# Four output products per pair, without the sums of the way back from the rotated frame, in a state-space mixer

## The chip, the cores and the metric

The kernel runs on one core of a Trainium2 chip. Its time is the device time of one execution in microseconds (us); the median of several runs is compared.

## What is computed

One sequence of 512 positions with 1024 channels passes a state-space (S5) layer, a SwiGLU feed-forward layer, a latent attention layer and a second feed-forward layer, all in float32. The change lies in the S5 layer. Cut to it:

```python
u = (h @ w_in).reshape(seq, 64 groups, 16)
a_re, a_im = decay * cos(li * step), decay * sin(li * step)
bu_re = einsum('gnk,lgk->lgn', br, u);  bu_im = einsum('gnk,lgk->lgn', bi, u)
xr, xi = associative_scan over positions of x[l] = a * x[l-1] + bu[l]      # complex
y = einsum('gkn,lgn->lgk', cr, xr) - einsum('gkn,lgn->lgk', ci, xi)
z = gelu(y + d_skip * u)
val, gate = split(z @ w_glu);  x = x + val * sigmoid(gate)
```

## The kernel before, in words

Positions are handled in blocks of `T` = 4, so that the scan runs over `C` = 128 blocks. The 64 groups of 64 states form 32 pairs that fill the 128 partitions; eight chunks t = 0..7 hold four pairs each (`PPC`). A complex recurrence is made real by turning every state into a frame that rotates with it: the inputs are turned by cosine and sine tables (`Cs`, `Sn`, made in `rotor`, L529), a real scan with the decay `RH` follows, and the result is turned back.

`s5_core` (L297) writes these steps per chunk:

- `turn_u` (L585) and `turn_w` (L576): transposes on TensorE (PE), evacuated by ScalarE (ACT) into `uT` and `WT`.
- `scan` (L594): PE makes the block inputs (L606) in two PSUM banks; VectorE (DVE) multiplies each bank by `Cs` and `Sn` (`pc`, `qc`, L612), adds them to `z` (L614, L615), scans the two parts (L617), multiplies `z` by `Cs` and `Sn` (`xpc`, `xqc`, L622) and sums these products to the real and the imaginary state `X` (L623, L624).
- `taps` (L544): small products for the part of the output that stays inside a block, evacuated by ACT into `Tb`.
- `outputs` (L626): four products of `uT` with `Tb` (L633), then two products for each of four pairs, `X` real and imaginary against the output weights `Obd` (L638). ACT applies the GELU and writes `Y` (L641). A product of two float32 operands shows as two MATMUL records in the profile.
- `coefs` (L492): DVE forms the weights `W` and `E`; ACT copies `E` into the block-diagonal `Obd` (L517), twice per chunk.
- `turn_y` (L644): `Y` is transposed on PE; ACT and DVE split it into `zh` and `zl`.
- `partial` (L653): 12 products of a finished chunk with the first gate weights, in the four `ps_g` banks.

The loop at L693 writes, for t, the steps `turn_u`, `turn_w`, `scan`, `taps` of chunk t+1, then `outputs` of t, `coefs` of t+2 and `turn_y` of t. The order in which each engine runs them is not the written one: a scheduler with a model of the times sets it when the program is built, and each engine then runs its list strictly in that order. The tiles `X`, `Obd`, `Tb`, `RH` have two buffers (chunk parity, `NB`), `z` has two, `pc` and `qc` one. The PSUM tag `x` has four banks taken in turn, so that a chunk's products wait for the readers of earlier ones. After the core, PE runs the remaining 288 gate products of the layer without a break.

Of the kernel before, what the change touches and what calls it, by code (L numbers as in the profile page):

```python
# [16 lines left out]
P = 128  # L17
# [5 lines left out]
T = 4  # L23
# [65 lines left out]
class Trunk:  # L89
# [207 lines left out]
    def s5_core(self, st):  # L297
# [44 lines left out]
        sqs = []  # L342
        for k in range(KD):
            if k % 2 == 0:
                two = cp.tile([P, 2, S], F32, name="xsq", tag=("z", "z", "pc", "qc")[k // 2], bufs=2 if k < 4 else 1)
            sqs.append(two[:, k % 2])
            nc.scalar.activation(out=sqs[k], in_=self.x[:, k], func=AF.Square)
        ups = {0: [self.ps("x") for _ in range(T)]}
# [18 lines left out]
        def tt(out, x, y, op, eng=v):  # L367
            eng.tensor_tensor(out=out, in0=x, in1=y, op=op)
# [102 lines left out]
        Wz = [lp.tile([P, 2 * PPC, 5, 16], F32, name=f"Wz{i}") for i in range(NB)]  # L471
        Tb = [lp.tile([P, 2, 2, 2, T, 16], F32, name=f"Tb{i}") for i in range(NB)]
        Obd = [lp.tile([P, 2 * PPC, T, 2, 16], F32, name=f"Obd{i}") for i in range(NB)]
        X = [lp.tile([P, 2, PPC, C], F32, name=f"X{i}") for i in range(NB)]
        RH = [lp.tile([P, PPC, C], F32, name=f"RH{i}") for i in range(NB)]
        for b in range(NB):
            g.memset(Wz[b], 0.0)
            g.memset(X[b][:, :, :, 0:1], 0.0)
            g.memset(RH[b][:, :, 0:1], 0.0)
        for z in Tb + Obd:  # L480
            g.memset(z, 0.0)

        Us, coef, states, rotors, zs, gps = {}, {}, {}, {}, [], []
# [8 lines left out]
        def coefs(t):  # L492

            bc = bcs_.pop(t)
            if t + 3 < NCT:
                load_bc(t + 3)

            def weigh(o, j, n, re, im):
                def bb(x):
                    return x.unsqueeze(2).broadcast_to([P, 2 * PPC, n, 16])  # L500

                def gg(x):
                    return x[:, 2 * t:2 * t + 2].rearrange("p a c (e j) -> p (a c e) j", e=2).unsqueeze(3).broadcast_to([P, 2 * PPC, n, 16])

                ma, mb = (cp.tile([P, 2 * PPC, n, 16], F32, name="w" + z, tag="e" + z, bufs=1) for z in "ab")
                tt(ma, bb(bc[:, j]), gg(re), M_)
                tt(mb, bb(bc[:, j + 1]), gg(im), M_)
                tt(o, ma, mb, A_)

            W = cp.tile([P, 2 * PPC, T, 16], F32, name="W", bufs=1)  # L510
            weigh(W, 0, T, GrS, GiS)
            nc.scalar.activation(out=Wz[t % NB][:, :, 1:5:2], in_=W[:, :, 0:1, :].broadcast_to([P, 2 * PPC, 2, 16]), func=AF.Copy)
            E = cp.tile([P, 2 * PPC, T + 1, 16], F32, name="E")
            weigh(E, 2, T + 1, ArS, AiN)
            for g2 in range(2):
                h = slice(64 * g2, 64 * g2 + 64)
                nc.scalar.activation(out=Obd[t % NB][h, :, :, g2], in_=E[h, :, 1:], func=AF.Copy)  # L517
            coef[t] = {"W": W, "E": E}

        def turns_of(t, o, j, start, stop):  # L520
# [73 lines left out]
        def scan(t):  # L594

            b = t % NB
            (Sn, Cs), WT, uT = rotors[t], coef[t]["WT"], states[t]
            nc.scalar.activation(out=RH[b][:, :, 1:].rearrange("p (e a) c -> p e a c", e=2),
                                 in_=rho[:, t * PPC:(t + 1) * PPC].rearrange("p (a e) -> p e a", e=2).unsqueeze(3).broadcast_to([P, 2, 2, C - 1]), func=AF.Copy)
            ps_v = [self.ps("x") for _ in range(2)]  # L600
            for q in range(2):
                for c in range(2):
                    for g2 in range(2):
                        for e in range(2):
                            h = slice(64 * e, 64 * e + 64)
                            nc.tensor.matmul(out=ps_v[e][64 * g2:64 * g2 + 64, (2 * q + c) * C:(2 * q + c + 1) * C],  # L606
                                             lhsT=WT[h, q, c, 64 * g2:64 * g2 + 64], rhs=uT[h, q, g2], start=True, stop=True)
            pc, qc = (cp.tile([P, 2, PPC, C], F32, name=n, bufs=1) for n in ("pc", "qc"))
            for e in range(2):
                vv = ps_v[e].rearrange("p (a c k) -> p c a k", a=2, c=2)  # L610
                for o, w in ((pc, Cs), (qc, Sn)):
                    tt(o[:, :, 2 * e:2 * e + 2], vv, w[:, 2 * e:2 * e + 2].unsqueeze(1).broadcast_to([P, 2, 2, C]), M_)  # L612
            z = cp.tile([P, 2, PPC, C], F32, name="z")
            tt(z[:, 0], pc[:, 0], qc[:, 1], A_)  # L614
            tt(z[:, 1], pc[:, 1], qc[:, 0], S_)  # L615
            for c in range(2):
                v.tensor_tensor_scan(out=z[:, c].rearrange("p a b -> p (a b)"), data0=RH[b].rearrange("p a b -> p (a b)"),  # L617
                                     data1=z[:, c].rearrange("p a b -> p (a b)"), initial=0.0, op0=M_, op1=A_)
            n = C - 1
            xc, xs = (cp.tile([P, 2, PPC, C], F32, name="x" + m, tag=m, bufs=1) for m in ("pc", "qc"))  # L620
            for o, w in ((xc, Cs), (xs, Sn)):
                tt(o[:, :, :, :n], z[:, :, :, :n], w[:, :, :n].unsqueeze(1).broadcast_to([P, 2, PPC, n]), M_)  # L622
            tt(X[b][:, 0, :, 1:], xc[:, 0, :, :n], xs[:, 1, :, :n], S_)  # L623
            tt(X[b][:, 1, :, 1:], xc[:, 1, :, :n], xs[:, 0, :, :n], A_)  # L624

        def outputs(t):  # L626

            b = t % NB
            uT = states.pop(t)
            ps_y = self.ps("x")  # L630
            for q in range(2):
                for g2 in range(2):
                    nc.tensor.matmul(out=ps_y.rearrange("p (q e j g k) -> p q g e j k", q=2, e=2, j=T, g=2)[:, q, g2], lhsT=uT[:, q, g2],  # L633
                                     rhs=Tb[t % NB][:, q, g2].rearrange("p e j k -> p (e j k)"), start=q == 0 and g2 == 0, stop=False, skip_group_check=True)
            for q in range(2):
                for e in range(2):
                    for c in range(2):
                        nc.tensor.matmul(out=ps_y[:, (2 * q + e) * P:(2 * q + e + 1) * P], lhsT=X[b][:, c, 2 * e + q],  # L638
                                         rhs=Obd[b][:, 4 * q + 2 * c + e].rearrange("p j g k -> p (j g k)"), start=False, stop=c == 1, skip_group_check=True)
            Y = cp.tile([P, T, PPC, 32], F32, name="Y", bufs=1)  # L640
            nc.scalar.activation(out=Y.rearrange("p j a k -> p a j k"), in_=ps_y.rearrange("p (a j k) -> p a j k", a=PPC, j=T), func=AF.Gelu_apprx_tanh)  # L641
            states[t] = Y
# [36 lines left out]
        rotor(0)  # L679
        taps(0)  # L680
        scan(0)
        rotor(1)
        coefs(1)

# [6 lines left out]
            whole_turns(t)  # L691
            rotor(t)
        for t in range(NCT):  # L693
            for f, d in ((turn_u, 1), (turn_w, 1), (scan, 1), (taps, 1), (outputs, 0), (coefs, 2), (turn_y, 0)):
                if 0 <= t + d < NCT:
                    f(t + d)
                if f is scan and t in (1, 3):
# [461 lines left out]
```

## Time and profile before

| | before |
|---|---|
| median of 3 runs | 1229.52 us (1227.26 to 1230.77) |
| the profiled execution | 1228.52 us, of which the span from the first to the last instruction is 1226.7 us |
| PE matmul busy | 1182.0 us (96%) |
| PE weight load busy | 959.8 us (78%) |
| DVE busy | 664.2 us (54%) |
| ACT busy | 489.2 us (40%) |
| mean granted TensorE clock | 0.979 of full speed |

The shares are means over stages of quite different kinds. The S5 core lies in about the first 200 us of the span; the rest is mostly feed-forward and attention, where PE is busy throughout. Windows of the trace are therefore read stage by stage, and the waits of PE within them.

### The profile page before, as it was taken

To read this page: it belongs to the slowest core of one execution; us is meant where nothing else is said; L and a number is where in the kernel's file an instruction comes from. 1 tells how busy PE (TensorE), PEld (TensorE's weight loads), DVE (VectorE), ACT (ScalarE), POOL (GpSimd) and SP (SyncE) were. 2 spreads that over 40 slices of the span, in tenths; PEclk is the share of its full clock that TensorE was granted. 3 is DMA by queue.
4 is the path that set the end of the run, shared out by engine and by line. 5 is a ranking of instruction groups with operands and counts; after the bars stand their busy time and mean duration, and the time that the engine had idled before them with its cause. 6 is when DMAs were issued, how large, how long until landed. Compare 5 with 4: busy or idle time off the path is not lost.

```text
span 1226.7 us, 15533 instructions
## 1 busy us (share of the span) xinstructions
PE 1182.0 (96%) x6133; PEld 959.8 (78%) x6136; DVE 664.2 (54%) x1194; ACT 489.2 (40%) x821; POOL 137.2 (11%) x149
## 2 busy tenths in 40 slices
PE   7977999999999999999999898999999999999998
PEld 6766777888888888888878676667888888888887
DVE  7797894357444444333358767744844444443221
ACT  7646444254232232233245766644432332322110
POOL 0300000030000000000234445432100000000000
PEclk9978799999999999999999899999999999999999
DMA  6210012323333233333222101103233232333331
GB/s 230 69 27 27 28 36 86 103 86 104 91 98 103 92 97 99 95 95 95 86 88 67 37 2 41 52 2 103 86 103 103 87 103 91 99 99 103 120 114 46
DMA packets 31896, 100.96 MB, mean 82 GB/s; under 512 B 3664, under 2 KB 4688, under 8 KB 31824
## 3 DMA queue, kind: packets, MB, share of 16 engines
q1 hardware_dynamic: 31680, 99.97, 26.2%
q8 instruction: 48, 0.79, 0.3%
q14 instruction: 24, 0.20, 0.1%
q10 hardware_dynamic: 144, 0.00, 0.0%
HBM read 97.86 MB, written 2.10 MB: 81 GB/s over the span
## 4 chain that ended last, share of the span: by engine, by line
PE 83%; DVE 9%; ACT 4%; issue 2%; POOL 1%; DMA 1%; SPq 0%; DVEq 0%; ACTq 0%
PE ps_ps L155 20%; PE ps_ps L154 20%; PE ps_ps L153 19%; PE ps_s L965 2%; PE ps_x L153 2%; PE ps_x L155 2%; PE ps_x L154 2%; PE ps_a L153 2%; PE ps_a L154 2%; PE ps_a L155 2%; DVE wl L142 1%; PE ps_x L638 1%; PE ps_g L153 1%; PE ps_x L606 1%; PE ps_po L1002 1%
## 5 line engine op out<-in xcount | busy, mean ns | idle before, releaser
L141 ACT ACTIVATE wh<-w 128x1024 fp32r<-128x1024 f32 (+3 forms) x193 | 191.3, 993 | 548.0 <-PE ps_ps L154 351.0
L142 DVE TENSOR_TENSOR wl<-w,wh 128x1024 fp32r<-128x1024 f32 (+3 forms) x193 | 221.9, 1151 | 212.8 <-ACT wh L141 212.7
L153 PE MATMUL ps_ps<-fh,wh 128*128 128x512 f32 x704 | 274.2, 390 | 0.0
L155 PE MATMUL ps_ps<-fh,wl 128*128 128x512 f32 x704 | 273.4, 389 | 0.0
L154 PE MATMUL ps_ps<-fl,wh 128*128 128x512 f32 x704 | 273.4, 389 | 0.0
L154 PEld LDWEIGHTS ps_ps<-fl,wh 128*128 128x128 f32 x704 | 132.1, 188 | 28.1 <-issue 0.5
L153 PEld LDWEIGHTS ps_ps<-fh,wh 128*128 128x128 f32 x704 | 132.1, 188 | 27.6 <-issue 0.5
L155 PEld LDWEIGHTS ps_ps<-fh,wl 128*128 128x128 f32 x704 | 132.1, 188 | 27.5
L153 PE MATMUL ps_ps<-ah,wh 128*128 128x512 f32 x352 | 136.9, 389 | 0.0
L154 PE MATMUL ps_ps<-al,wh 128*128 128x512 f32 x352 | 136.9, 389 | 0.0
L155 PE MATMUL ps_ps<-ah,wl 128*128 128x512 f32 x352 | 136.9, 389 | 0.0
L743 DVE TENSOR_TENSOR ut<-ps_ps,rstd 128x512 f32<-128x512 f32 x44 | 30.4, 691 | 127.8 <-PE ps_ps L155 127.8
L263 POOL TENSOR_TENSOR acc<-acc,sq 128x512 f32<-128x512 f32 x21 | 30.5, 1452 | 564.6 <-ACT sq L258 316.0
L153 PEld LDWEIGHTS ps_ps<-ah,wh 128*128 128x128 f32 x352 | 66.1, 188 | 13.8
L154 PEld LDWEIGHTS ps_ps<-al,wh 128*128 128x128 f32 x352 | 66.1, 188 | 13.8
L155 PEld LDWEIGHTS ps_ps<-ah,wl 128*128 128x128 f32 x352 | 66.1, 188 | 13.5
L740 DVE TENSOR_TENSOR gt<-ps_ps,rstd 128x512 f32<-128x512 f32 x44 | 30.4, 691 | 83.2 <-PE ps_ps L155 83.1
L973 POOL TENSOR_SCALAR p<-p,sm 128x128 f32<-128x128 f32 (+2 forms) x48 | 45.8, 960 | 70.6 <-DVE sm L971 59.3
L965 PE MATMUL ps_s<-kT,qT 96*128 96x384 f32 (+3 forms) x128 | 46.6, 466 | 1.5 <-ACT p L970 1.5
L970 ACT ACTIVATE p<-ps_s,mx 128x128 f32<-128x128 f32 (+3 forms) x64 | 33.4, 525 | 22.8 <-DVE mx L968 18.6
L168 ACT ACTIVATE ah<-ut 128x512 fp32r<-128x512 f32 x44 | 27.9, 634 | 30.7 <-DVE ut L744 30.7
L968 DVE TENSOR_REDUCE mx<-ps_s 128x1 f32<-128x128 f32 (+3 forms) x64 | 30.8, 486 | 15.1 <-PE ps_s L966 14.6
(384 smaller groups left out, 1756.1 us busy)
## 6 DMA issues: line engine op xcount, KB each, us to landing
w<-w_gu SPq DMA_DIRECT2D x88, 512.0 KB, 3.5
w<-w_down SPq DMA_DIRECT2D x32, 512.0 KB, 3.5
w<-w_glu SPq DMA_DIRECT2D x12, 512.0 KB, 3.5
w<-w_down SPq DMA_DIRECT2D x16, 384.0 KB, 3.1
w<-w_in SPq DMA_DIRECT2D x7, 512.0 KB, 3.6
w<-w_o SPq DMA_DIRECT2D x6, 512.0 KB, 3.2
x<-xT SPq DMA_DIRECT2D x8, 256.0 KB, 6.0
bc<-ssm_bc SPq DMA_DIRECT2D x8, 256.0 KB, 2.8
```

Of the source, the lines that this page charges most:

```text
L141: nc.scalar.activation(out=wh[:, c], in_=w[:, c], func=AF.Copy)
L142: nc.vector.tensor_tensor(out=wl[:, c], in0=w[:, c], in1=wh[:, c].bitcast(F32), op=ALU.subtract)
L153: nc.tensor.matmul(out=out, lhsT=lh, rhs=rh, start=start, stop=False)
L154: nc.tensor.matmul(out=out, lhsT=lh, rhs=rl, start=False, stop=False)
L155: nc.tensor.matmul(out=out, lhsT=ll, rhs=rh, start=False, stop=stop)
L263: nc.gpsimd.tensor_tensor(out=acc, in0=acc, in1=sq, op=ALU.add)
L740: v.tensor_tensor(out=gt, in0=pss[0], in1=rstd, op=ALU.mult)
L743: v.tensor_tensor(out=ut, in0=pss[1], in1=rstd, op=ALU.mult)
L965: nc.tensor.matmul(out=ps, lhsT=qT[:, i * P:n], rhs=kT[:, 0:n], start=True, stop=False)
L968: v.reduce_max(out=m1, in_=ps, axis=AX.X, negate=True)
L970: nc.scalar.activation(out=pb, in_=ps, func=AF.Exp, bias=m1, accum_out=s1)
L973: eng.tensor_scalar(out=pb, in0=pb, scalar1=s1, scalar2=None, op0=M_)
```

## The change

The two DVE sums that made `X` from `xpc` and `xqc` are gone. The products of `z` with the cosine (`XC`) and the sine (`XS`) go to PE as they are, and `outputs` makes four products per pair: the real part of `XC` and the imaginary part of `XC`, with the weights that `X` had; the real part of `XS` with the weights of the imaginary part; the imaginary part of `XS` with the negated weights `On`, a new tile that ACT copies from `E` with scale -1 (twice per chunk). `XC` and `XS` have one buffer each, `z` has one instead of two, and the turning back is a step of its own, `rotate`, written after `outputs` of the chunk before. Two more fills on GpSimd (POOL) zero `On`.

```diff
+        On = [lp.tile([P, PPC, T, 2, 16], F32, name=f"On{i}") for i in range(NB)]
-        X = [lp.tile([P, 2, PPC, C], F32, name=f"X{i}") for i in range(NB)]
+        XC, XS = (lp.tile([P, 2, PPC, C], F32, name=m) for m in ("XC", "XS"))
...
                 nc.scalar.activation(out=Obd[t % NB][h, :, :, g2], in_=E[h, :, 1:], func=AF.Copy)
+                nc.scalar.activation(out=On[t % NB].rearrange("p (a e) j g k -> p a e j g k", e=2)[h, :, :, :, g2],
+                                     in_=E.rearrange("p (a c e) j k -> p c a e j k", a=2, c=2)[h, 0, :, :, 1:], func=AF.Copy, scale=-1.0)
...
-            z = cp.tile([P, 2, PPC, C], F32, name="z")
+            z = cp.tile([P, 2, PPC, C], F32, name="z", bufs=1)
...
-            xc, xs = (cp.tile([P, 2, PPC, C], F32, name="x" + m, tag=m, bufs=1) for m in ("pc", "qc"))
-            for o, w in ((xc, Cs), (xs, Sn)):
-                tt(o[:, :, :, :n], z[:, :, :, :n], w[:, :, :n].unsqueeze(1).broadcast_to([P, 2, PPC, n]), M_)
-            tt(X[b][:, 0, :, 1:], xc[:, 0, :, :n], xs[:, 1, :, :n], S_)
-            tt(X[b][:, 1, :, 1:], xc[:, 1, :, :n], xs[:, 0, :, :n], A_)
+            states[t] = (uT, z)
+
+        def rotate(t):
+            (Sn, Cs), n = rotors[t], C - 1
+            states[t], z = states[t]
+            for o, w in ((XC, Cs), (XS, Sn)):
+                tt(o[:, :, :, 1:], z[:, :, :, :n], w[:, :, :n].unsqueeze(1).broadcast_to([P, 2, PPC, n]), M_)
...
-                    for c in range(2):
-                        nc.tensor.matmul(out=ps_y[:, (2 * q + e) * P:(2 * q + e + 1) * P], lhsT=X[b][:, c, 2 * e + q],
-                                         rhs=Obd[b][:, 4 * q + 2 * c + e].rearrange("p j g k -> p (j g k)"), start=False, stop=c == 1, skip_group_check=True)
+                    r = 4 * q + e
+                    for i, (lhs, rhs) in enumerate(((XC[:, 0], Obd[b][:, r]), (XC[:, 1], Obd[b][:, r + 2]), (XS[:, 0], Obd[b][:, r + 2]), (XS[:, 1], On[b][:, 2 * q + e]))):
+                        nc.tensor.matmul(out=ps_y[:, (2 * q + e) * P:(2 * q + e + 1) * P], lhsT=lhs[:, 2 * e + q],
+                                         rhs=rhs.rearrange("p j g k -> p (j g k)"), start=False, stop=i == 3, skip_group_check=True)
...
-            for f, d in ((turn_u, 1), (turn_w, 1), (scan, 1), (taps, 1), (outputs, 0), (coefs, 2), (turn_y, 0)):
+            for f, d in ((turn_u, 1), (turn_w, 1), (scan, 1), (taps, 1), (outputs, 0), (rotate, 1), (coefs, 2), (turn_y, 0)):
```

Because the scheduler sets the order, the lists of the engines differ in more than the diff shows. Three places matter below.

The first is ACT around the GELU of chunk 0 (`Y`, L641 before, L649 now); `Obd` is refilled for chunk 2, `WT` is the input of the scan of chunk 2. Before:

```order
L598 ACTIVATE RH_486<-dr 128x4x127
L641 ACT_TABLE_LOAD
L641 ACTIVATE Y<-ps_x 128x4x4x32
L517 ACTIVATE Obd_481<-E 64x32x16 x2
L591 ACTIVATE uT<-ps_x 128x512
L582 ACTIVATE WT<-ps_x 128x512
L168 ACTIVATE zh_890<-ps_x 128x512
```

Now:

```order
L595 ACTIVATE uT<-ps_x 128x512
L602 ACTIVATE RH_488<-dr 128x4x127
L519 ACTIVATE Obd_481<-E 64x32x16 x2
L649 ACT_TABLE_LOAD
L649 ACTIVATE Y<-ps_x 128x4x4x32
L520 ACTIVATE On_483<-E 64x16x16 x2
L586 ACTIVATE WT<-ps_x 128x512
L168 ACTIVATE zh_900<-ps_x 128x512
```

`uT` moved ahead of the end of `outputs`; the refill of `Obd`, which needs `outputs` to be over with the old one, moved ahead of the GELU; the pair of `On` copies stands between `Y` and `WT`.

The second is PE around the outputs of chunk 3 (L633 and L638 before, L640 and L646 now), with the two halves of the scan inputs of chunk 4 (L606 before, L610 now). Before:

```order
L606 MATMUL ps_x<-uT,WT 64x128 x8
L521 MATMUL ps_x<-counts,turned 128x512
L153 MATMUL ps_g<-zh_1287,wh 128x512 x4
L633 MATMUL ps_x<-Tb_480,uT 128x8x16 x4
L638 MATMUL ps_x<-Obd_482,X_484 128x128 x8
L606 MATMUL ps_x<-uT,WT 64x128 x8
```

Now:

```order
L610 MATMUL ps_x<-uT,WT 64x128 x8
L525 MATMUL ps_x<-counts,turned 128x512
L153 MATMUL ps_g<-zh_1309,wh 128x512 x4
L640 MATMUL ps_x<-Tb_480,uT 128x8x16 x4
L646 MATMUL ps_x<-Obd_482,XC 128x128 x2
L646 MATMUL ps_x<-Obd_482,XS 128x128
L646 MATMUL ps_x<-On_484,XS 128x128
L646 MATMUL ps_x<-Obd_482,XC 128x128 x2
L646 MATMUL ps_x<-Obd_482,XS 128x128
L610 MATMUL ps_x<-uT,WT 64x128 x8
```

The second half of the scan inputs now stands behind 7 of the 16 output products, where it stood behind all 8.

The third is DVE between the input of chunk 4's scan (`scan`) and its turning back (`rotate` now). Before:

```order
L368 TENSOR_TENSOR E<-wa,wb 128x640
L368 TENSOR_TENSOR pc<-ps_x,Cs 128x2x256
L368 TENSOR_TENSOR qc<-ps_x,Sn 128x2x256
L368 TENSOR_TENSOR wa<-bc,GrS 128x512
L368 TENSOR_TENSOR wb<-bc,GiS 128x512
L368 TENSOR_TENSOR z<-pc,qc 128x512 x2
L142 TENSOR_TENSOR wl<-w,wh 128x512
L169 TENSOR_TENSOR zl_1436<-ps_x,zh_1435 128x512
L617 SCALAR_TENSOR_TENSOR z<-RH_485,z 128x512 x2
```

Now:

```order
L368 TENSOR_TENSOR E<-wa,wb 128x640
L368 TENSOR_TENSOR wa<-bc,GrS 128x512
L368 TENSOR_TENSOR wb<-bc,GiS 128x512
L368 TENSOR_TENSOR pc<-ps_x,Cs 128x2x256
L368 TENSOR_TENSOR qc<-ps_x,Sn 128x2x256
L368 TENSOR_TENSOR z<-pc,qc 128x512 x2
L621 SCALAR_TENSOR_TENSOR z<-RH_487,z 128x512 x2
L368 TENSOR_TENSOR XC<-z,Cs 128x8x127
L368 TENSOR_TENSOR XS<-z,Sn 128x8x127
L169 TENSOR_TENSOR zl_1464<-ps_x,zh_1463 128x512
```

Four operations (`wa`, `wb`, `wl`, `zl`) no longer stand between the second `pc` and the scan.

## Rows read from the trace of the kernel before

**Rows 1.** By stretch: length, busy us (x count) PE, PEld, DVE, ACT, POOL, PEclk, DMA.
```profile
63.00:139.00 76.00, 63.29 (x661) 53.89 (x661) 64.65 (x88) 41.05 (x92) 0.00 (x0) 0.80 0.09 25
139.00:157.90 18.90, 15.62 (x157) 13.16 (x156) 17.33 (x24) 12.80 (x26) 0.00 (x0) 0.82 0.09 29
157.90:200.00 42.10, 41.23 (x361) 34.49 (x362) 31.86 (x55) 19.08 (x40) 0.00 (x0) 1.00 0.13 39
280.00:500.00 220.00, 220.00 (x973) 182.15 (x972) 109.19 (x134) 69.07 (x85) 0.00 (x0) 1.00 0.31 97
```
**Rows 2.** Waits of PE from 63 to 157.9: us in total, times, longest.
```profile
PE ps_x L648 <- ACT Y L641: 4.4, 3, 2.7
PE ps_x L558 <- ACT uT L591: 3.1, 1, 3.1
PE ps_x L606 <- ACT WT L582: 2.5, 2, 1.6
PE ps_x L580 <- ACT ab L540: 2.2, 1, 2.2
...
PE ps_x L633 <- DVE qc L368: 0.4, 1, 0.4
```
**Rows 3.** Stretches at the lower clock: the first of five, and their sum.
```profile
68.40:78.20 9.80, 9.80 (x119) 9.54 (x119) 9.01 (x15) 5.56 (x16) 0.00 (x0) 0.50 0.21 55
...
sum 36.80, PE 36.36 PEld 32.89 DVE 32.76 ACT 13.89 POOL 0.00; mean PE 7.27 PEld 6.58 DVE 6.55 ACT 2.78 POOL 0.00
```
**Rows 4.** The chain of waits, chunks 1 to 6: start us, us, what.
```profile
79.50 1.12 DVE z L617
...
81.29 1.28 ACT L641
...
89.97 2.62 PE ps_x L638 x14
...
116.48 1.80 PE ps_x L638 x16
...
128.54 2.35 PE ps_x L638 x16
...
151.08 3.02 PE ps_x L638 x16
...
170.84 1.29 DVE X L368 x2
```
**Rows 5.** PE in order of time: start us, us, what, around two chunks' outputs.
```profile
77.11 2.57 PE L638 MATMUL ps_x<-Obd,X 128*128 128x128 f32 x16
79.52 0.60 PE L590 MATMUL ps_x<-ctab,U 128*128 128x128 f32 x4
...
116.32 1.95 PE L638 MATMUL ps_x<-Obd,X 128*128 128x128 f32 x16
118.10 0.60 PE L580 MATMUL ps_x<-ctab,W 128*128 128x128 f32 x4
```
**Rows 6.** Groups from 60 to 190: count, busy us, mean ns, idle before.
```profile
L368 DVE TENSOR_TENSOR X<-xpc,xqc 128x508 f32<-128x508 f32 x16 | 10.2, 681 | 0.0
...
L517 ACT ACTIVATE Obd<-E 64x512 f32<-64x512 f32 x12 | 7.5, 623 | 0.1
...
L512 ACT ACTIVATE Wz<-W 128x256 f32<-128x256 f32 x6 | 2.5, 410 | 0.0
```
**Rows 7.** DVE in order of time, chunk 4's scan (in brackets: idle before).
```profile
131.97 0.69 DVE L368 TENSOR_TENSOR pc<-ps_x,Cs 128x512 f32<-128x512 f32 x1 [2.86 <-PE ps_x L606]
...
133.17 0.68 DVE L368 TENSOR_TENSOR wa<-bc,GrS 128x512 f32<-128x512 f32 x1
133.77 0.69 DVE L368 TENSOR_TENSOR wb<-bc,GiS 128x512 f32<-128x512 f32 x1
```
**Rows 8.** POOL's last fill of the core, and ACT's first copy into that tile.
```profile
40.78 1.85 POOL L481 MEMSET Obd<- 128x1024 f32 x2
...
44.80 1.28 ACT L517 ACTIVATE Obd<-E 64x512 f32<-64x512 f32 x2
```

More of the change, by code (lines that the diff above doesn't have):

```diff
@@ L344, in s5_core @@
             if k % 2 == 0:
-                two = cp.tile([P, 2, S], F32, name="xsq", tag=("z", "z", "pc", "qc")[k // 2], bufs=2 if k < 4 else 1)
+                two = cp.tile([P, 2, S], F32, name="xsq", tag=("z", "U", "pc", "qc")[k // 2], bufs=2 if k // 2 == 1 else 1)
             sqs.append(two[:, k % 2])
@@ L477, in s5_core @@
             g.memset(Wz[b], 0.0)
-            g.memset(X[b][:, :, :, 0:1], 0.0)
             g.memset(RH[b][:, :, 0:1], 0.0)
-        for z in Tb + Obd:
+        for z in (XC, XS):
+            g.memset(z[:, :, :, 0:1], 0.0)
+        for z in Tb + Obd + On:
             g.memset(z, 0.0)
@@ L618, in scan @@
                                      data1=z[:, c].rearrange("p a b -> p (a b)"), initial=0.0, op0=M_, op1=A_)
-            n = C - 1
-            xc, xs = (cp.tile([P, 2, PPC, C], F32, name="x" + m, tag=m, bufs=1) for m in ("pc", "qc"))
-            for o, w in ((xc, Cs), (xs, Sn)):
-                tt(o[:, :, :, :n], z[:, :, :, :n], w[:, :, :n].unsqueeze(1).broadcast_to([P, 2, PPC, n]), M_)
-            tt(X[b][:, 0, :, 1:], xc[:, 0, :, :n], xs[:, 1, :, :n], S_)
-            tt(X[b][:, 1, :, 1:], xc[:, 1, :, :n], xs[:, 0, :, :n], A_)
+            states[t] = (uT, z)
[4 more added lines that the diff above has]
+                tt(o[:, :, :, 1:], z[:, :, :, :n], w[:, :, :n].unsqueeze(1).broadcast_to([P, 2, PPC, n]), M_)
         def outputs(t):
@@ L681, in s5_core @@
         scan(0)
+        rotate(0)
         rotor(1)
```

## Prediction

> **What bounds the kernel now.** Read the busy time by stretch first [rows 1]. From 280 to 500 us PE is busy for 220 of 220 us: there only PE's own work counts, and the engines' lists of those stages are the same but for a few rows. The S5 core is different. From 63 to 157.9 us PE is busy for 63.29 + 15.62 = 78.9 of 94.9 us and its clock is low in between; from 157.9 to 200 it is busy for 41.23 of 42.1 at full clock, and so on to the end of the layer. So the core has two parts: one with waits up to 157.9, and one after it in which PE already has its work end to end. DVE is close to full as well: 17.33 of 18.9 us just before 157.9.
>
> Next, who holds PE in the first part [rows 2]. The nine rows of that view come to 15.8 us; ACT ends 14.9 of them in six rows (the GELU `Y`, `uT`, `WT`, and `ab` of the rotor), DVE 1.0 in three, of which 0.4 is the longest. PE also runs at half speed in five stretches, 36.8 us together, whose clock is about 0.50, i.e. 1.2 of 2.4 GHz [rows 3]; that costs 36.8 / 2 = 18.4 us of work. Each such stretch follows a wait of PE on ACT.
>
> Last, the chain of waits [rows 4]. It passes through the output products L638 of chunks 1, 2, 3 and 4, goes from there through ACT (table load, `Y`, `Obd`, `WT`) to the scan inputs of the chunk after next, and back. The sums that the change drops stand on it once, at 170.84. The reader should see that DVE is busy but not what the others wait for, and that the output products, which are doubled, are.
>
> **The change, part by part.** *Dropped sums.* Sixteen additions of 128x508 at 10.2 us of busy time; an operation of this size starts the next one 0.60 later (133.17 and 133.77), so DVE loses 16 x 0.6 = 9.6 us of work [rows 6, 7]. `XC` and `XS` have the shape of the old products and cost the same.
>
> *Added products.* Eight per chunk, two records each: 16 records took 118.10 - 116.32 = 1.78 us at full clock [rows 5]. So 8 x 1.78 = 14.2 us of PE. At half clock the chain shows 3.02 for the same 16, mixed; the added ones stand last in their group, where the clock has mostly risen, so I take 1.8. The bounds of a group are 1.8 and 3.0.
>
> *Added copies.* Two `On` copies per chunk of 64x256. The nearest rows are `Wz`, 128x256 at 0.41, and `Obd`, 64x512 at 0.62 [rows 6]; the length of a partition's row is that of `Wz`, so 0.41 each, 0.8 a chunk, at most 1.2. In chunks 1, 2 and 4 they lie between `Y` and what PE waits for.
>
> *Fills.* Two more on POOL, half as long as `Obd`'s, which take 1.85 for two and end at 42.6; ACT comes to that kind of copy at 44.80 [rows 8], so a microsecond more is covered. Without that cover the first scan would start up to 1 us later.
>
> *Order and buffers.* `XC` and `XS` have one buffer: `rotate` of t+1 waits for the outputs of t. Behind it on DVE stand `W`, `zl` and the next `pc`, for which `turn_w`, the gate products and the next scan wait. `z` with one buffer costs nothing, since its only reader, `rotate`, is ahead of the next `z` on the same engine.
>
> *The sum, first part (to 157.9), by chunk.* Chunk 0: the outputs ended at 79.52, and ACT, which waited for the scan of chunk 1 (to 80.6), began its table load at 81.29 [rows 4, 5]. They now end 1.8 + 0.5 later (the four transposes of `U` moved ahead of them), at 81.8, or 0.5 past that; `On` adds 0.8, and `uT`, now ahead, gives back about 0.5, a copy between `Wz` and `Obd` in time: +0.8. Chunk 1: 1.8 + 0.8 = +2.6, all on the chain. Chunk 2: the same 2.6, and 24 instead of 20 gate products ahead of the next scan's inputs, 4 x 220 / 973 = 0.9 [rows 1]: +3.5. Chunk 3: the second half of the scan inputs now waits for 7 products instead of 8, -0.2; on DVE `wa`, `wb`, `wl` and `zl` no longer follow the second `pc` but fill its wait of 2.86 or come later, 4 x 0.6 [rows 7]: -2.4. Chunk 4: +2.6. Together 0.8 + 2.6 + 3.5 - 2.6 + 2.6 = **+6.9 us** at the point where PE's unbroken work begins, and from there on it is the same work but for three chunks' added products.
>
> *Second part.* Chunks 5, 6 and 7 add 3 x 1.78 = 5.3 us to an engine that has 42.10 - 41.23 = 0.9 us left [rows 1]: **+4.4 us**. DVE's gain of 4 x 1.2 there (four chunks from 139 on) is not what PE waits for.
>
> Sum: 6.9 + 4.4 = 11.3 on the profiled execution's 1228.5, or 1239.8; I take **1239.5**, since small orders that I could not follow (a scheduler that packs its lists again) rather give than take. The profiled execution is 1.0 below the median of the three runs.
>
> A rule speaks against the second part. The Trainium skill's page Perfetto Trace Analysis, section Identifying the Most-Contended Engine, says that matmul busy time is a bad measure of what PE has left, and that the busy share of the weight loads is the one to read. By it PE has room: 34.49 of 42.1 us, 82%, so that the 5.3 us would fit and the sum would be 1235.4. The trace disagrees: in the feed-forward stretch, where matmuls follow each other without a gap, the same share is 182.15 of 220, 83% [rows 1], so 82% is full here and the rule gets no chance of its own.
>
> **The rivals.** *A, the added products lie in PE's waits up to 157.9.* PE has 15.8 us of waits there and needs 5 x 1.8 = 9.0. Then only the second part is paid: 1228.5 + 4.4 = 1232.9. For it: the room is there. Against it: the waits come after the outputs, on ACT's `Y` and `WT`, which start only when the outputs end; the added products push a wait, they don't fill it. It decides if ACT's start is set by something else than the outputs, as it is in chunk 0.
>
> *B, DVE was the bound: faster.* DVE has only 1.6 us free from 139 to 157.9 [rows 1], and 9.6 us fall away. If DVE set the pace of all chunks, 9.6 would come off and 4.4 be added: 1223.3. It decides if PE's products wait for `pc`/`qc` or `X` rather than for ACT. Against it: DVE ends only 1 us of PE's waits [rows 2], and itself waits for PE's scan inputs (2.86 at 131.97) [rows 7].
>
> *C, PE keeps its clock.* If the denser work of PE spared two of the five stretches at the lower clock, 2 x 36.8 / 5 / 2 = 7.4 us would come back: 1232.1; all five, 18.4, give 1221.1. Against it: each stretch starts after a wait on ACT [rows 2, 3] that the change lengthens. The Trainium skill's page TensorE: Matmul & The Clock Gate, Part 1, says that the throttled clock is the default and that activity releases it. By that rule more products in a gap would help; the trace shows all five stretches behind gaps that the change leaves.
>
> *D, the single buffer bites.* The scan of chunk 1 ends at 80.6 and the lengthened outputs of chunk 0 at 81.8 [rows 4, 5], so `rotate` waits there by 1 us; if it waits like that or by 2 in the chunks that follow, beyond what the sum holds, and one more stretch at the lower clock follows in chunk 6, 36.8 / 5 / 2 = 3.7 us, the time is near 1228.5 + 11.3 + 3.7 + 2 = 1245.5.
>
> That the sums are not really dropped is no case: the list of DVE has 16 fewer additions.
>
> **How the numbers follow.** About 0.3% (3.7 us) is what a measurement of this kernel can tell from no change, so 1225.8 to 1233.2 counts as the same. Forecast 0.52 (its own range 1234 to 1245); A 0.17, B 0.08, C 0.08, D 0.15. Faster: B and a third of C, 0.11. Same: A and a third of C, 0.20. Slower: the rest, 0.69. The range 1228 to 1247 takes in A, the forecast, D and half of C; it leaves out B, the rest of C and a tail above, under 0.2. With `On` at 0.62 and a group at 3.0 in the three chunks of the chain, the sum would be 1.2 + 3.6 higher, 1244.6, which the range holds.
>
> **What the profile would show.** L646 with 256 records and 1.8 us more per group; PE's matmul and load time each longer. The waits of PE on `Y`, `WT` and `uT` no smaller; five stretches at the lower clock. DVE busy 9 to 10 us less, with new waits: `XC` on the output products, `pc` and `zl` longer. PE's unbroken work begins near 165 instead of 157.9, and the layer's last gate product ends some 11 us later; behind it all stages last as long as before. I am wrong if the waits of PE shrink by more than 5 us, if fewer stretches are slow, or if the end of the layer moves by less than 4 us.

## The result, and the profile after

The changed kernel took **1244.48 us** (median of 4 runs, 1239.11 to 1249.12) beside 1228.76 for the kernel before (4 runs, 1227.26 to 1230.77): ratio 1.0132, 95% interval 1.0108 to 1.0156. Measured again beside other kernels (run e5) it was 1244.81 us, ratio 1.0140 (1.0122 to 1.0157). The forecast was 1239.5, its range 1228 to 1247. The sign and the range held; the terms behind the number, as the experiments show, did not all hold, and part of the agreement is luck.

The profiled execution of the changed kernel took 1242.62 us (span 1240.8), 14.1 more than that of before. First the busy time by stretch: us, then PE, weight loads, DVE, ACT, POOL busy with the number of instructions, PE's granted clock, DMA share, GB/s.

```profile
63.00:139.00 76.00, 61.62 (x634) 52.74 (x633) 58.90 (x79) 40.65 (x91) 0.00 (x0) 0.84 0.08 22
139.00:173.00 34.00, 27.74 (x347) 24.85 (x346) 26.31 (x34) 20.65 (x45) 0.00 (x0) 0.83 0.07 25
173.00:216.00 43.00, 42.84 (x343) 38.42 (x342) 26.43 (x46) 20.21 (x41) 0.00 (x0) 0.97 0.13 40
296.00:516.00 220.00, 220.00 (x972) 182.16 (x971) 107.59 (x132) 69.42 (x86) 0.00 (x0) 1.00 0.32 98
```

Beside [rows 1]: in the feed-forward stretch PE is busy for 220 of 220 us, as before. PE's unbroken work, which began at 157.9, now begins at 165.8, but at half the clock until 175 (below). The first product of the feed-forward layer moved from 255.38 to 269.75, by 14.4: the whole difference lies ahead of it.

Not all of that belongs to the change. ACT's first copy of `GrS`, ahead of anything that the diff touches in the core, started at 37.59 before and at 40.18 after, because two loads took longer (`ctab` by 1.2, `w` by 1.5 us). In e5, the same kernel, it started at 39.24, and in e1 at 38.11: this is scatter between executions. So I count from that copy to the first feed-forward product, once for each kernel (the columns of the view above):

```profile
37.59:255.38 217.79, 200.24 (x1622) 166.97 (x1623) 158.14 (x227) 109.94 (x222) 4.41 (x13) 0.91 0.19 55
```

```profile
40.18:269.75 229.57, 208.78 (x1752) 178.93 (x1751) 150.04 (x211) 116.37 (x238) 5.34 (x15) 0.92 0.17 52
```

217.79 became 229.57: **+11.8 us**. The table divides this time for each profiled execution. PE's busy time and granted clock were read in 200 equal slices of it; "work" is the sum of busy x clock, "low clock" the sum of busy x (1 - clock), "waits" the time less the busy time. The three add up to the time, to rounding.

```
kernel                       its run   time    work   low clock   waits
before                       1228.5   217.8   181.9     18.3      17.5
after                        1242.6   229.6   192.0     16.8      20.8
e5  after again              1245.2   233.2   190.9     23.5      18.8
e1  before, products twice   1236.5   225.9   193.0     16.9      16.0
e2  before, no sums          1222.0   211.2   180.5     12.7      17.9
e3  order alone              1230.8   218.5   182.1     20.0      16.3
e4  after, no On             1247.3   235.2   192.7     23.9      18.6
e6  e4 with two buffers      1234.9   225.5   191.5     19.8      14.2
e7  e6, rotate in scan       1232.5   221.8   192.2     15.1      14.5
e8  coef. sums on GpSimd     1228.0   217.9   183.7      9.3      25.0
e9  before, no coef. sums    1223.6   211.2   180.8     16.4      14.0
e10 before, twice late       1230.0   219.3   186.5     15.0      17.8
e11 work in the gaps         1229.5   217.5   184.2     16.2      17.0
e12 three buffers of RH      1226.9   216.6   180.8     18.1      17.7
```

Each row is one execution and can lie off the median of its kernel: e4's is the longest of its six (1234.7 to 1247.3), e2's too, and e1's (1236.5) is near the shortest of 1236.2 to 1243.6. From before to after, work grew by 10.1 and waits by 3.3; the low clock cost 1.5 less in this run, but 5.2 more in e5. The growth of the work goes with the added products, but it is less than the 14.2 us that the prediction counted for them; the measure is a rough one (in e11 added transposes are busy for 6.3 us and raise it by 2.3). The groups of the output products from 60 to 215 us (group, count, busy us, mean ns of one, idle before):

```profile
L646 PE MATMUL ps_x<-Obd,XC 128*128 128x128 f32 x128 | 20.6, 286 | 0.0
L646 PE MATMUL ps_x<-On,XS 128*128 128x128 f32 x64 | 12.8, 283 | 0.0
L646 PE MATMUL ps_x<-Obd,XS 128*128 128x128 f32 x64 | 12.8, 282 | 0.0
```

They are 256 records where there were 128, four kinds per pair. Next the waits of PE from 63 to 175 (us in total, times, longest):

```profile
PE ps_x L656 <- ACT Y L649: 8.2, 3, 3.0
PE ps_x L640 <- DVE qc L368: 3.3, 2, 2.5
PE ps_x L584 <- DVE zl L169: 2.8, 1, 2.8
PE ps_x L610 <- ACT WT L586: 2.4, 4, 0.8
PE ps_x L584 <- ACT ab L544: 2.2, 1, 2.2
PE ps_x L562 <- ACT uT L595: 0.8, 1, 0.8
```

Against [rows 2], `Y` rose from 4.4 to 8.2, and DVE, which ended 1.0 us of PE's waits, now ends 6.3, 2.8 of it by `zl` ahead of the transposes of `W`. On DVE itself the new wait is the one on the single buffer (in brackets: idle before, and what ended it):

```profile
160.84 1.22 DVE L368 TENSOR_TENSOR XC<-z,Cs 128x1016 f32<-128x1016 f32 x1 [1.08 <-PE ps_x L646]
...
178.50 1.22 DVE L368 TENSOR_TENSOR XC<-z,Cs 128x1016 f32<-128x1016 f32 x1 [1.92 <-PE ps_x L646]
```

And between the outputs of chunks 4 and 5, where chunk 6's scan inputs are made, stands a stretch at the lower level, 1.2 GHz, that the kernel before did not have: ten microseconds with PE at work for 9.2 (columns as in the first fence).

```profile
165.00:175.00 10.00, 9.21 (x114) 8.90 (x115) 6.35 (x10) 4.03 (x13) 0.00 (x0) 0.50 0.01 2
```

### The profile page after: what moved, and what is told of

The parts are those of the page before. It is cut to its first block, busy times and chain, and to the rows that moved or that the text cites. A ratio compares the mean times of both kernels' runs of the same rounds, so it can differ in the third digit from the quotient of the medians.

```text
span 1240.8 us, 15799 instructions
## 1 busy us (share of the span) xinstructions
PE 1190.7 (96%) x6264; PEld 972.0 (78%) x6264; DVE 658.9 (53%) x1178; ACT 494.5 (40%) x837; POOL 135.6 (11%) x151
## 4 chain that ended last, share of the span: by engine, by line
PE 85%; DVE 7%; ACT 4%; issue 1%; POOL 1%; DMA 1%; SPq 0%; DVEq 0%; ACTq 0%
PE ps_ps L153 19%; PE ps_ps L155 19%; PE ps_ps L154 19%; PE ps_s L974 2%; PE ps_x L646 2%; PE ps_x L153 2%; PE ps_x L155 2%; PE ps_x L154 2%; PE ps_a L153 2%; PE ps_a L154 2%; PE ps_a L155 2%; PE ps_po L1011 1%; PE ps_g L153 1%; PE ps_x L610 1%; PE ps_a L959 1%
## 5 line engine op out<-in xcount | busy, mean ns | idle before, releaser
L142 DVE TENSOR_TENSOR wl<-w,wh 128x1024 fp32r<-128x1024 f32 (+3 forms) x193 | 224.8, 1166 | 215.9 <-ACT wh L141 215.7
L154 PEld LDWEIGHTS ps_ps<-al,wh 128*128 128x128 f32 x352 | 66.1, 188 | 13.8
```

Source lines behind the costliest of these rows:

```text
L142: nc.vector.tensor_tensor(out=wl[:, c], in0=w[:, c], in1=wh[:, c].bitcast(F32), op=ALU.subtract)
L154: nc.tensor.matmul(out=out, lhsT=lh, rhs=rl, start=False, stop=False)
```

## The experiments

All ratios are against the kernel before, measured beside each; microseconds are the ratio less 1, times 1228, and differ from the difference of the medians by up to 0.9. One thing holds for all of them: a scheduler writes each engine's list from its own simulated times, so that an edit comes with a list that is packed again. One list matters below, ACT's, and it is read from the traces.

**e1, the products alone.**

```diff
-  Obd[..] <- E
-  for c in (0, 1):        ps_y += X[c] . Obd[4q+2c+e]
+  Obd[..] <- 0.5 * E
+  for c in (0, 1, 0, 1):  ps_y += X[c] . Obd[4q+2c+e]
```

> The kernel before, with each of its eight output products per chunk made twice (Obd halved by the scale of its copy, so that two of them add up to one); the sums, the order of the loop and the buffers stay as they were, and no On copy is made. Theory (the added products are the cost: 1.8 us in chunks 1, 2 and 4, 0.5 in chunk 0, 4.4 us in chunks 5 to 7): +9.5 to +10.5 us over before, about 1239. Rival buffer and order (the products mostly fit in PE's waits, and the wait of XC on the outputs, the moved rotate and the On copies make the rest): about +4.4, 1233. Rival clock (the added cost is the slow stretch in chunk 6, which the new order brought): under +6, and no stretch at 0.50 behind 165 us.

Measured: 1238.5 us, ratio 1.0090 (1.0069 to 1.0112), **+11.1 us**. The theory's band was 9.5 to 10.5; both rivals, at +4.4 and under +6, are outside the interval (8.5 to 13.8). By the table, whose execution shows 8.1 of it, PE's work grew by 11.1; 1.5 of it came back in waits and 1.4 through the clock. A low stretch came at the same place here too (159 to 169 us, clock 0.54), without the new order: the order does not make it.

**e2, the sums alone.**

```diff
-  xpc = z * Cs ; xqc = z * Sn
-  X[0] = xpc[0] - xqc[1] ; X[1] = xpc[1] + xqc[0]
+  xqc = z * Sn ; X = z * Cs
```

> The kernel before without the two sums per chunk: the product with the cosine goes straight into X, the product with the sine is made and not read (this leaves the sums out of the computation). Nothing else is changed: eight products, order, two buffers of X. Theory (DVE is busy, but its sums are not what the others wait for): -2.5 to +0.5 us against before. Rival B (DVE sets the pace): -6 to -10 us.

Measured: 1218.77 us, ratio 0.9921 (0.9906 to 0.9936), **-9.7 us**. My theory falls; the number is rival B's. But B's mechanism (DVE holds PE) is not what the table shows: PE's waits are 17.9 beside 17.5, its work is 180.5, and 5.6 us come from the clock (this execution, at 1222.0, shows 6.6 of the 9.7). The place is the stretch from 95 to 111 us. Before, and then e2:

```profile
95.00:111.00 16.00, 12.79 (x106) 10.05 (x108) 12.12 (x15) 12.85 (x30) 0.00 (x0) 0.79 0.07 17
```

```profile
95.00:111.00 16.00, 15.24 (x196) 12.18 (x193) 14.47 (x21) 13.71 (x35) 0.00 (x0) 1.00 0.13 35
```

Before, PE works 12.8 of 16 us at a mean clock of 0.79; in e2 15.2 at 1.00. ACT's list differs there. Before, ACT in order of time, then what PE did:

```profile
98.14 1.28 ACT L539 ACT_TABLE_LOAD   x1
...
100.59 0.58 ACT L168 ACTIVATE zh<-ps_x 128x512 fp32r<-128x512 f32 x1
...
101.55 0.60 ACT L591 ACTIVATE uT<-ps_x 128x512 f32<-128x512 f32 x1
```

```profile
102.20 1.90 PE L558 MATMUL ps_x<-E,Wz 64*64 64x64 f32 x32 [3.06 <-ACT uT L591]
```

The sine table load and `Sn`, `RH`, `zh`, `ab` stand ahead of `uT`; PE waits 3.06 for `uT`, and the third of the five stretches at the lower clock follows. In e2 the same engine reads:

```profile
96.39 0.60 ACT L168 ACTIVATE zh<-ps_x 128x512 fp32r<-128x512 f32 x1
96.89 0.59 ACT L591 ACTIVATE uT<-ps_x 128x512 f32<-128x512 f32 x1
...
99.94 1.28 ACT L539 ACT_TABLE_LOAD   x1
```

Here `zh`, `uT` and `U` stand ahead of the table load, at 96.89 instead of 101.55, and from 87 to 110 us PE has no wait over 0.4. So the scheduler, with the sums gone, wrote another list. How much of the 9.7 is that list and how much DVE's time, this run does not tell.

**e9, as much off DVE at another place.**

```diff
-  tt(mb, bc[j+1], im) ; tt(o, ma, mb, add)
+  tt(o, bc[j+1], im)
```

> The kernel before without the sums of the coefficients: the second product goes straight into W and E (this leaves those two sums per chunk out of the computation). It takes 0.60 + 0.73 us per chunk off DVE, 8 in 8 chunks, slightly more than the sums of the way back (9.6), but not between scan and products, and with nothing put on GpSimd. If DVE's load is what counts: -6 to -10 us against before, the clock at 0.985 or more as in e2_before_no_sums. If the place of the sums counts (between z and the output products): -3 to +1 us, the clock near 0.979.

Measured: 1224.59 us, ratio 0.9969 (0.9958 to 0.9979), **-3.8 us**, clock by run 0.979 to 0.984. The interval, -5.2 to -2.6, leaves out "DVE's load is what counts" and reaches the edge of "the place of the sums counts" (-3 to +1). Its list of ACT is of e2's kind (`uT` at 95.89, the table load at 98.95), so that this list and 10.6 us less of DVE are here together worth 3.8, and cannot by themselves account for the 9.7 of e2. In the profiled execution the waits are 3.5 lower, and the low clock costs 1.9 less.

**e8, the same load moved to GpSimd.**

```diff
-  tt(o, ma, mb, add)                 # DVE
+  gpsimd.tensor_tensor(o, ma, mb, add)
```

> The kernel before, with the two sums of the coefficients per chunk (W 128x512, E 128x640) made by GpSimd in place of DVE; the core's sums and eight products stay. It takes off DVE 8 x (0.6 + 0.73) = 10.6 us, about as much as the sums of the way back, and adds no PE work. If what counts is DVE's load and not that chain of sums: -6 to -10 us against before, 1218 to 1222, under both kernels. If the sums counted because z, X and the products follow each other, or GpSimd is slow at it and W comes late: -1 to +5 us.

Measured: 1227.59 us, ratio 0.9991 (0.9981 to 1.0002): no change that can be told, at the edge of the second expectation. It is not that nothing happened: the clock by run rose to 0.984 to 0.989, and in the table the low clock costs 9.0 less while PE's waits are 7.5 longer. Nor was DVE's load lowered, as the run was to do: DVE did not get the time back. Two products and the sums of e8 on DVE, then GpSimd's sums beside them:

```profile
98.05 2.12 DVE L368 TENSOR_TENSOR xpc<-z,Cs 128x1016 f32<-128x1016 f32 x1
100.09 1.21 DVE L368 TENSOR_TENSOR xqc<-z,Sn 128x1016 f32<-128x1016 f32 x1
...
102.69 2.64 DVE L368 TENSOR_TENSOR X<-xpc,xqc 128x508 f32<-128x508 f32 x2
```

```profile
97.78 1.31 POOL L508 TENSOR_TENSOR W<-wa,wb 128x512 f32<-128x512 f32 x1 [10.08 <-PE ps_x L580]
102.84 1.94 POOL L508 TENSOR_TENSOR E<-wa,wb 128x640 f32<-128x640 f32 x1 [3.75 <-DVE wb L368]
```

The product with the cosine takes 2.12 where the one with the sine behind it takes 1.21, and two sums take 2.64 where one group takes 1.29 in [rows 4]; both lie beside a sum of GpSimd, of which the second takes 1.94. The Trainium skill's page Perfetto Trace Analysis, section Optimizing Scalar/DVE Operations, says that GpSimd and DVE share a read port of SBUF, so that work moved between them may not help; these rows agree.

**e3, the order alone.**

```diff
-  scan: ... X <- sums            # inside scan, X in two buffers
+  rotate(t+1): X <- sums         # behind outputs(t), X and z in one buffer
```

> The order and the buffers of the changed kernel, with the arithmetic of the kernel before: the way back and its sums stand in rotate behind the outputs, X and z have one buffer, eight products per chunk, no On copies. Theory: the order gives +0.9 (24 gate products), -0.5 (uT) and about -2 in chunk 3, but the sums now stand behind the outputs on DVE, four more instructions of 0.6 between XC and W: -2 to +3 us against before. Rival buffer and order: +5 to +9 us, most of what the changed kernel lost.

Measured: 1227.45 us, ratio 0.9998 (0.9986 to 1.0010), **-0.2 us**. With eight products the moved way back and its single buffer cost nothing. Taken alone this would have closed the case of the buffer; e6 opens it again.

**e5, the changed kernel again,** no edit.

> The changed kernel as it is, measured again beside the others of this call. All theories: its first four runs lay between 1239.1 and 1249.1, so a median of 1240 to 1247, and a mean granted clock of 0.972 to 0.983 by run, as there.

Measured as given above; its clock by run was 0.972 to 0.975. It was measured beside e6 and e7. The next run, e4, was measured on another chip, so that e4 is compared with these through the ratios to the kernel before.

**e4, without On.**

```diff
-  On <- -1 * E ; XS = z * Sn ; fourth product XS[1] . On
+  XS[0] = z[0] * Sn ; XS[1] = (z[1] * -1) * Sn ; fourth product XS[1] . Obd[r]
```

> The changed kernel without the On copies: the sign is put into XS by writing its second half as (z times -1) times Sn, in one instruction, so XS takes two instructions of 128x508 in place of one of 128x1016, and the fourth product reads Obd. Four products per pair as in the changed kernel. Theory (0.8 us of On lie on the chain in chunks 0, 1, 2 and 4): -2.5 to -3.5 us against the changed kernel, +8 to +13 against before, with the products' cost left. Rival (the copies lie in waits of ACT): within 1 us of the changed kernel.

Measured: 1240.67 us (1234.69 to 1247.25), ratio 1.0102 (1.0075 to 1.0128). Against e5 that is 0.0038 or **-4.7 us**, with an uncertainty of about 3.9 (both half-widths, squared and added). Against the first measurement of the changed kernel (1.0132) it is -3.7, with an uncertainty of 4.4, so that no gain at all lies inside it too. It fits the theory and the 3.2 of the prediction, but the rival's "within 1 us" is not ruled out; and the traces do not show where the gain lies, since e4's execution, its longest, took longer than both of the changed kernel.

**e6, two buffers.**

```diff
-  XC, XS: one buffer ; WT: two
+  XC, XS: two buffers ; WT: one
```

> The changed kernel without On (sign put into XS) and with two buffers of XC and XS, so that rotate of a chunk does not wait for the outputs of the chunk before (WT gets one buffer to make the space). The order of the loop stays. Theory buffer (the single buffer holds DVE and undoes what the dropped sums give): 1230 to 1235, some 7 us under the version without On and with one buffer (1240.7). Theory products (with the products doubled PE is late whatever DVE does): within 2.5 us of 1240.7, since XC waited for the products by 3.0 us in all in the changed kernel's trace.

Measured: 1234.62 us, ratio 1.0046 (1.0032 to 1.0061); against e4 0.0056 or **-6.9 us**, uncertainty about 3.7. The theory of the buffer holds, the other is out. DVE's waits from 62 to 200 (us in total, times, longest), e4 and then e6, which has none at `XC`:

```profile
DVE pc L368 <- PE ps_x L607: 15.2, 8, 3.8
...
DVE XC L368 <- PE ps_x L644: 5.6, 3, 2.2
```

```profile
DVE wl L142 <- ACT wh L141: 10.4, 6, 3.7
DVE pc L368 <- PE ps_x L607: 6.2, 7, 1.8
```

5.6 us of waiting at `XC`, and 15.2 instead of 6.2 at `pc` behind it. Part of this can be that e4's execution was its longest (12.4 us above e6's, where the ratios make it 6.9). And the scheduler's list for ACT turns with the buffer. ACT in e4, and the wait of PE that follows:

```profile
107.08 1.28 ACT L540 ACT_TABLE_LOAD   x1
...
109.34 0.60 ACT L168 ACTIVATE zh<-ps_x 128x512 fp32r<-128x512 f32 x1
...
110.29 0.63 ACT L592 ACTIVATE uT<-ps_x 128x512 f32<-128x512 f32 x1
```

```profile
110.72 1.11 PE L581 MATMUL ps_x<-ctab,W 128*128 128x128 f32 x4 [4.20 <-DVE zl L169]
```

ACT in e6:

```profile
100.40 0.60 ACT L168 ACTIVATE zh<-ps_x 128x512 fp32r<-128x512 f32 x1
100.90 0.59 ACT L592 ACTIVATE uT<-ps_x 128x512 f32<-128x512 f32 x1
...
102.96 1.28 ACT L540 ACT_TABLE_LOAD   x1
```

e4 has the table load ahead of `zh` and `uT`, and PE waits 4.20 for `zl`, which DVE makes from `zh`; e6 has it behind them, and no such wait. The changed kernel has e4's kind (table load 102.06, `zh` 103.85, a wait of 2.80).

**e7, the arithmetic alone.**

```diff
-  rotate(t+1) behind outputs(t)
+  XC, XS written inside scan, as X was
```

> The kernel of e6_no_on_two_buffers with rotate back in the place of the kernel before, inside scan, ahead of taps and outputs: what is left of the change is its arithmetic alone (sums dropped, sixteen products). If the two parts add up as they measured alone (products +10.4, sums -9.3): 1229 +- 2. Theory products (the gain of the sums does not stand once the products are doubled): 1236 to 1241. Theory order (the moved rotate is the loss): at least 6 us under e6_no_on_two_buffers.

Measured: 1232.37 us, ratio 1.0039 (1.0023 to 1.0054), **+4.8 us** (2.8 to 6.6) over before; against e6 0.9, within its uncertainty: the order is no loss here either. (e6 and e7 keep XS in two instructions and one buffer of WT.) The interval leaves out 1236 and more, "the gain of the sums does not stand". Adding e1 and e2 gives +1.4, 3.4 less than measured, but with the uncertainties of all three runs (3.7 together) this does not show that the parts fail to add up. Most of the sums' gain, 11.1 - 4.8 = 6.3 of 9.7 (uncertainty 3.3), stands beside sixteen products.

**e10, the late products alone.**

```diff
+  if t >= 5: as e1, else as before
```

> The kernel before with its output products made twice in chunks 5, 6 and 7 only (Obd halved there). The prediction's second term says 3 x 1.78 - 0.9 = +4.4 us, all of it PE time in a stretch where PE has no waits; that leaves 10.4 - 4.4 = 6.0 us for chunks 0 to 4. Rival (the late chunks' products fit, the whole 10.4 us came from chunks 0 to 4): under +2 us. Rival (the late chunks pay more, a further stretch at the lower clock): +7 or more.

Measured: 1230.31 us, ratio 1.0018 (1.0006 to 1.0031), **+2.2 us** (0.7 to 3.8): between the forecast's 4.4 and the rival's "under 2". The time of the whole program misleads here. Up to the outputs of chunk 5 each engine's list is the same in both kernels; the added products come after it. From ACT's first copy of `GrS` to the first output product of chunk 5, and from there to the feed-forward layer, before and then e10 (columns as in the first fence):

```profile
37.59:165.59 128.00, 111.98 (x1127) 93.66 (x1129) 108.50 (x156) 76.07 (x171) 4.41 (x13) 0.85 0.11 31
165.59:255.38 89.79, 88.26 (x497) 73.31 (x495) 49.63 (x72) 33.87 (x51) 0.00 (x0) 1.00 0.29 89
```

```profile
37.91:162.94 125.03, 108.46 (x1128) 90.58 (x1126) 107.77 (x155) 75.95 (x171) 4.08 (x10) 0.88 0.11 31
162.94:257.22 94.28, 93.11 (x544) 78.32 (x543) 50.33 (x73) 33.84 (x51) 0.00 (x0) 1.00 0.28 84
```

Where the products were added, the time grew by 94.28 - 89.79 = 4.5 us: the forecast's 4.4. Ahead of it, where the lists are the same, it fell by 3.0, and there the clock is 0.88 beside 0.85 (last section). If the parts of e1 add up, chunks 0 to 4 hold some 6.6 of its 11.1.

**e11, work put into the gaps.**

```diff
   ps_z = bank()
+  for j in range(10 if t < 5 else 0): transpose(ps_z, ident)
   for j in range(4): transpose(ps_z, Y[j])
```

> The kernel before with ten more 128x128 transposes of the identity (1.6 us at full clock) ahead of the transposes of Y in chunks 0 to 4, into the same bank, which the real ones then write over; nothing reads them. They stand where PE waits for the GELU. If work in a gap keeps the clock (rival C): PE's clock rises to 0.984 or more by run, and -3 to -8 us against before, under both kernels. If the clock falls all the same, they are 5 x 1.6 us of work, of which some 4 lie in waits: +2 to +5 us.

Measured: 1226.70 us, ratio 0.9990 (0.9976 to 1.0004): no change that can be told; mean clock by run 0.983 (0.980 to 0.985), under the 0.984 that rival C was to show. ACT's list again turned to e2's kind, so what the filler itself gave is not separated. Of the kernels with such a list it is the one with eight products and DVE's work in full.

**e12, three buffers of RH.**

```diff
-  RH[t % 2]
+  RH[t % 3]
```

> The kernel before with three buffers of RH (the decay that the scan reads, copied by ACT) in place of two. In the trace of before ACT waits 8.3 us in three places for DVE's scan at this copy, and the table load and Y, for which PE waits, stand behind it (at 80.65 for 4.29 us). If this is the way by which DVE's sums reach PE: -2 to -6 us against before, under both kernels, and no wait of ACT at RH. If ACT would have waited there for the output products all the same, or the moved order takes it back: -1.5 to +1.5 us.

Measured: 1226.13 us, ratio 0.9978 (0.9967 to 0.9988), -2.7 us. It did not test what it was made for. The scheduler put each `RH` copy a chunk earlier, where it waits for the same scan (ACT's waits, 62 to 160; the same 8.3, 3 and 4.3 as in the kernel before):

```profile
ACT RH L599 <- DVE z L618: 8.3, 3, 4.3
```

Whether DVE's scan reaches PE through this copy stays open. Where the 2.7 us come from is open too: the profiled execution shows 1.2 of them in the stretch of the table and 1.0 behind it (last section). It is the fastest kernel that computes all, but by less than the 0.3% that counts here.

## Why the prediction was right in sign and range, and where it was wrong

The steps, with what the runs give for each; they add up from before to after along e7, e6, e4 and e5, by construction. The forecast's column is its sum, grouped by cause: products 0.5 in chunk 0, 1.8 in chunks 1, 2 and 4 and 4.4 in the last three; `On` 0.8 in four chunks; order -0.5, +0.9, -0.2 and -2.4.

```
step                           forecast          measured (us)
added products                 +10.3             +11.1 (e1); late part 4.5 for 4.4 (e10)
dropped sums                    0 (9.6 hidden)   -9.7 (e2); -6.3 beside the products (e7 - e1)
  arithmetic together          +10.3             +4.8 (e7)
order of the loop              -2.2              +0.9 (e6 - e7), -0.2 (e3)
single buffer                   0 (in rival D)   +6.9 (e4 - e6)
On copies                      +3.2              +4.7 (e5 - e4)
sum                            +11.3             +17.2 (e5)
```

*Added products: right.* They do not fit in PE's waits: rival A, 1232.9, is refuted by e1, where PE still waits for 16.0 us (17.5 before). The term for chunks 5 to 7, 3 x 1.78 = 5.3 less 0.9 of room, was right to 0.1 us in e10's trace, and that those products fit (1235.4) is refuted with it.

*Dropped sums: wrong.* The step that failed is "DVE loses 16 x 0.6 = 9.6 us of work", entered as nothing because DVE ended 1.0 us of PE's waits [rows 2]. That view names what came last at each wait; it does not say what the list of the engine that came last would be if another had less to do. In e2 ACT's list did change, and PE's wait of 3.06 for `uT` went with it; but e9, with a list of that kind and at least as much taken off DVE (144.7 us busy, e2 149.2), gained 3.8 only, and e11, with such a list and DVE's work as before, 1.2 (-0.5 to 2.9). What makes the rest of the 9.7 is not shown; that these sums stand between the scan and the output products, and e9's do not, is the rival that is left.

*Order and buffers: wrong.* The sum has no term for the single buffer; "`rotate` waits there by 1 us" stands in rival D alone. It was measured at 6.9 (uncertainty 3.7). The waits at `XC` themselves are of the size that rival D gave (1.08 and 1.92 in the changed kernel). With one buffer ACT's list also has the table load ahead of `zh` and `uT`, which the prediction left out; how much of the 6.9 that is, no run shows. The order's -2.2 was not seen: +0.9 (uncertainty 2.6) and -0.2. e3 shows that the same single buffer costs nothing with eight products; that it bites with sixteen because they read it longer is argued from `XC`'s waits, not shown by itself.

*On copies: right* in size, within a wide interval (-0.8 to -8.6 for their removal).

So two wrong terms of opposite sign, 6 to 7 us each, left the sum near: the mechanism of the products was right, that the number came out in the range was in good part luck. **Rival D**, at 1245.5 with a chance of 0.15, describes the trace better than the forecast: `XC` waits by 1 and 2 us, and one more low stretch stands in chunk 6. Of D too the price was right more than the cause, since e1 has that stretch without the single buffer. **Rival C** got nothing: the low clock cost 16.8 and 23.5 beside 18.3.

*What the profile was to show.* L646 with 256 records: so. PE's work 14.2 us more: 10.1 by the table. Five low stretches: five, 37.5 us of them as before, but not the same ones (the first is gone in this run, the one in chunk 6 is new; e5 has six). Waits on `Y`, `WT` and `uT` "no smaller": `Y` larger, `WT` as before, `uT` at the taps 0.8 instead of 3.1. DVE less busy by 9 to 10: by 8.1 (158.14 to 150.04). Layer's end 11 later: 14.4, of which 2.6 were scatter ahead of the core. None of the three signs of being wrong came.

**One reading of all kernels.** In ACT's list the sine table load near 100 us stands ahead of `uT` in before, after (and e5), e1, e3, e4, e10 and e12, and behind it in e2, e6, e7, e8, e9 and e11. The edits of e2, e6 and e9 turned the list and gained 9.7, 6.9 and 3.8; e8 and e11 turned it and gained nothing that can be told, but they also put work on GpSimd beside DVE, or on PE. This is a coincidence over 13 kernels, not a test: turning the list by hand, with nothing else changed, was not tried. How the 9.7 and the 6.9 divide between that list and DVE's own time stays open.

## What to carry to other kernels

A view that names the last releaser of each wait prices only edits that leave the lists of the other engines as they are; where a scheduler packs them again, price a freed engine from both sides, up to all of its work, and look at what the new lists do ahead of the late instruction. A trade of vector sums for matrix products is to be costed with its buffers: products that read an operand for twice as long can also hold its only buffer for longer, and what waits for it may turn another engine's list. Two of the four costs here, the sign copies and the single buffer, were not part of the arithmetic, and without them the trade cost 4.8 us instead of 17. And a difference of 2 or 3 us between two whole programs is to be looked for in the trace: compare first the stretches whose lists are the same, as in e10, where the edit's 4.5 us stood beside 3.0 that had nothing to do with where the edit was made.

## What the runs showed of the hardware that was not expected

*The same lists and waits, two clocks.* Up to 162 us before and e10 run the same lists, with the same waits of PE around chunk 3's scan inputs. PE before and then e10 (in brackets: idle before), then the stretch from the end of the first wait (columns as in the first fence):

```profile
120.29 0.66 PE L648 MATMUL ps_x<-ctab,Y 128*128 128x128 f32 x4 [1.36 <-ACT Y L641]
120.30:130.90 10.60, 8.97 (x51) 7.79 (x53) 8.81 (x13) 2.99 (x6) 0.00 (x0) 0.68 0.01 2
```

```profile
120.00 0.65 PE L649 MATMUL ps_x<-ctab,Y 128*128 128x128 f32 x4 [1.36 <-ACT Y L642]
120.00:130.60 10.60, 8.97 (x68) 7.54 (x69) 9.37 (x14) 4.51 (x9) 0.00 (x0) 0.84 0.01 2
```

PE is busy for 8.97 us in both, at 0.68 in one and 0.84 in the other, and gets through 51 and 68 records. It is not one odd run: the mean clock by run was 0.977 to 0.984 before (27 runs, mean 0.979) and 0.980 to 0.985 in e10 (12 runs, mean 0.983).

The same shows 450 us behind an edit, where before and e12 do the same work. PE's waits, before and then e12, and the stretch around them:

```profile
711.32 0.64 PE L950 MATMUL ps_a<-ctab,Qt 128*96 128x128 f32 x4 [1.15 <-POOL Qt L876]
712.74 0.66 PE L982 MATMUL ps_a<-ctab,p 128*128 128x128 f32 x4 [0.66 <-ACT qT L952]
710.00:718.00 8.00, 6.19 (x31) 4.96 (x31) 3.28 (x10) 4.41 (x10) 4.93 (x4) 0.79 0.00 0
```

```profile
711.12 0.64 PE L951 MATMUL ps_a<-ctab,Qt 128*96 128x128 f32 x4 [1.14 <-POOL Qt L877]
712.54 0.66 PE L983 MATMUL ps_a<-ctab,p 128*128 128x128 f32 x4 [0.67 <-ACT qT L953]
710.00:718.00 8.00, 6.08 (x42) 4.76 (x43) 3.74 (x12) 5.14 (x13) 5.67 (x6) 1.00 0.00 0
```

The waits agree to 0.01 us; the clock is 0.79 in one kernel, 1.00 in the other. Measured side by side, the mean clock by run was 0.976 to 0.981 before (17 runs, mean 0.979) and 0.980 to 0.985 in e12 (12 runs, mean 0.983), so it goes mostly with the kernel (single runs of before beside other kernels reach 0.985). Not all of it becomes time: behind the layer the low clock cost 6.0 us before and 2.7 in e12, but PE's waits were 19.0 and 20.7, and the whole stretch took 971.3 and 970.3. Within one kernel it also scatters: e6's runs lay between 0.978 and 0.990. What decides it, no run here shows; up to 3 us, as in e10, can be this alone.

*DVE beside GpSimd.* In e8 one DVE product became 0.9 us longer beside a GpSimd sum, and two sums 1.35, so that moving 1.33 us of sums per chunk off DVE freed next to nothing: from the first copy of `GrS` to the layer's end DVE was busy 157.0 us, beside 158.14 before.
